# Hyena norm ahead of the output projection, output tiles added from PSUM, output weights' low parts by DMA, query statistic by column sums

## The chip, the cores and the metric

The kernel runs on one core of a Trainium2 chip. A core has five engines that work through their own instruction queues: TensorE (PE in the profile, its weight loads PEld), VectorE (DVE), ScalarE (ACT), GpSimd (POOL) and SyncE (SP), which here only issues transfers. PE writes its results to PSUM, a memory of eight banks of 128 x 512 floats; everything else lies in SBUF. The metric is device time in microseconds (us) of one execution, as the median of several.

## The reference

One layer of an encoder on 512 tokens of width 1024, in float32. What matters here:

```
h = RMSNorm(x);  proj = h @ w_in      -> q-latent (768), kv-latent (256), shared rope key (32), Hyena x0, x1, v (3 x 512)
q = RMSNorm(c_q) @ w_uq;  k, v = RMSNorm(c_kv) @ w_ukv;  per-head RMSNorm of q and k, rope, softmax attention (8 heads)
y_hyena = x0 * long_conv(x1 * v)
y_mix = concat(RMSNorm(y_attn) * g_a, RMSNorm(y_hyena) * g_h)
x = x + y_mix @ w_out
x = x + (silu(g) * u) @ w_down        (gated MLP with a width-3 convolution)
x = x + sigmoid(x @ w_ple_gate) * RMSNorm(p @ w_ple)
```

RMSNorm divides by sqrt(mean(x^2) + 1e-6). Its scale is one number per token.

## The kernel before, in words

All matrices are kept transposed: 128 features on the partitions, 512 tokens along the row. A product of float32 values is made of three matmuls: each operand is split into a rounded high part `h` and the rest, the low part `l`, and h*h, h*l and l*h are summed (`prod3`). `split` (129) does this with one ACT copy and one DVE instruction.

Weights come as a stream of tiles of 128 x 1024 (`stream`, 149 to 157), always three tiles ahead of use. `wload` (137) takes one tile: SP fetches it raw (`wr`, 2 buffers), ACT rounds it into `wh` (3 buffers), and the low part `wl` (3 buffers) is made in one of two ways. Columns below `cut` are made by DVE as raw minus high (143). For columns above `cut`, ACT writes the negative rounded weights (145), and a transfer issued by POOL (146) fetches the same weights from DRAM once more and adds them on top. For the output weights `w_out` the cut is 512 of 1024.

PE's order is the order of the program, mixed by hand: `advance` and `spawn` put small tasks between the large products when a counted time is reached. The order on the other engines is made by a planner that takes what is ready by priority; `tc.high_priority` with the numbers of `PRI` shifts instructions ahead (positive) or back (negative). Tiles of PSUM come from two pools of four banks each, `mm_ps` and `ax_ps`; a tile waits until the one that had its bank is done with.

Around the change, in order of time:

- The first products: two kv-latent tiles (482) and the rope key by `in_gemm(2)` (495), all in `mm_ps`. Their evacuation (509, 511) waits for R1, the 1/rms of x. Then come twelve Hyena tiles (619) and six q-latent tiles (639), whose squares are added up in `accx`.
- `query_scale` (672): a matmul with ones adds `accx` over the partitions, eight equal rows of 512; `rows` copies eight rows to SBUF (667, ACT, priority 500); `turn_rows` (228) transposes them on PE into 32 columns, four token blocks of eight heads; `rms_cols` makes the statistic from them. `key_task` (686) does the same for the key's squares: sums by 688 and 690, a copy by 667, transposes. Both tasks run between the steps of the query projection (763).
- `gate` (827): for each of four tiles PE transposes the long convolution's result, DVE multiplies it into `x0`, ACT squares, POOL adds the squares in `acch`, and `x0` is split with the gain g_h (845, priority -300).
- The attention loop (981) with steps n = 0 to 36: scores of step n, transposes of the probabilities of step n-3 (`turn`), product with v (`weigh`), head output (`finish`). Gates stand at n = 4, 6, 7 and 9. At n = 10 `rms_bcast` (998) makes Rh, the 1/rms of the Hyena output, with a ones matmul (220) and `rsqrt` (203). At n = 16, 24 and 32 `hyena_out` (923) makes an output tile of the Hyena half; five more follow the loop. Since Rh is one number per token, it is applied after the projection: DVE multiplies the result by Rh (928) and adds x (929).
- Four output tiles before the end, Ra is made for the attention half in the same way (1005); its tiles are normed before the projection (1008), and 1016 adds the products of the attention half to the residual.

Of the kernel before, what the change touches and what calls it, by code (L numbers as in the profile page):

```python
# [14 lines left out]
AF = mybir.ActivationFunctionType  # L15
ALU = mybir.AluOpType
# [3 lines left out]
P = 128  # L20
# [19 lines left out]
D_RC = 1.5  # L40
# [7 lines left out]
TAIL = 'E0 P E1 R O S0 S1 V0 V1 S2 S3 V2 G0 V3'  # L48
ENG = {'pr0': 'G', 'a53': 'V', 'a64': 'V', 'sp3': 'V', 'pr2': 'G', 'sp7': 'G', 'qa2': 'V', 'm5': 'V', 'a51': 'G', 'ah1': 'G', 'hl0': 'V', 'fwo': 'G', 'ah3': 'G', 'qa5': 'V', 'hl2': 'G', 'qa3': 'V', 'm6': 'V', 'm7': 'G', 'm2': 'V', 'qa1': 'V', 'sp5': 'G', 'xt': 'V', 'Uc': 'G', 'sp4': 'G', 'w01': 'V', 'w11': 'V', 'a61': 'G', 'pr3': 'G', 'a67': 'G', 'a63': 'V', 'u4': 'G', 'a65': 'G', 'w10': 'G', 'u3': 'G', 'sp0': 'G', 'eos': 'V', 'vx': 'A', 'vl': 'V', 'vh': 'V', 'va': 'V', 'vf': 'V', 've': 'V', 'vc': 'A', 'sx': 'A', 'sl': 'V', 'sh': 'V', 'sa': 'V', 'sf': 'V', 'se': 'V', 'sc': 'V', 'qa4': 'G', 'sp6': 'V', 'm4': 'V', 'rot2': 'G', 'cv5': 'V', 'm1': 'G', 'a62': 'V', 'rot1': 'G'}
ATT = {'pr', 'a', 'ah', 'hl', 'xt'}  # L50
PRI = {'rows': 500, 'val': 20, 'kt': 60, 'rms': -120, 'cols': 400, 'H': 0, 'gate': 150, 'uT': -120, 'io': -20, 'sq': 20, 'turn': 0, 'so': -300, 'fold': -120, 't8': 0, 'gsq': -50, 'ie': 400}
QACT = 1
UQ = (2, 0, 4, 3, 5, 1)
D_KS = 5.0
# [3 lines left out]
RPRI = 0  # L58
LAG = 3
NPR = 4  # L60
FILLS = (16, 24, 32)
GN = (4, 6, 7, 9)
CPRI = 50
EPS = 1e-6
# [22 lines left out]
def tile_encoder_block(  # L87
# [9 lines left out]
    def e(key, default):  # L97
        if key.rstrip("0123456789") in ATT:
            return {"V": V, "G": G}[ENG.get(key, default)]
        return V  # L100

    def pri(key):
        return tc.high_priority(offset=PRI[key]) if PRI.get(key) else nullcontext()

# [9 lines left out]
    def mm_ps():  # L114
        return psm.tile([P, T], F32, tag="mm", name="mm")

    def ax_ps():
        return psx.tile([P, T], F32, tag="ax", name="ax")

    def atile(dt=F32R):  # L120
        return apool.tile([P, T], dt, tag="a", name="a")
# [4 lines left out]
    def f32(ap):  # L126
        return ap.bitcast(F32)

    def split(hi, lo, src, g=None):
        if g is None:  # L130
            S.activation(hi, src, AF.Copy)
            V.tensor_tensor(lo, src, f32(hi), op=ALU.subtract)
        else:
            S.activation(hi, src, AF.Copy, scale=g)
            V.scalar_tensor_tensor(lo, src, g, f32(hi), op0=ALU.mult, op1=ALU.subtract)

    def wload(src, n, cut):
        raw = wpool.tile([P, 1024], F32, tag="wr", name="wr", bufs=2)
        SP.dma_start(raw[:, :n], src)
        hi = wpool.tile([P, 1024], F32R, tag="wh", name="wh", bufs=3)  # L140
        lo = wpool.tile([P, 1024], F32R, tag="wl", name="wl", bufs=3)
        S.activation(hi[:, :n], raw[:, :n], AF.Copy)  # L142
        V.tensor_tensor(lo[:, :cut], raw[:, :cut], f32(hi[:, :cut]), op=ALU.subtract)  # L143
        if cut < n:
            S.activation(lo[:, cut:n], raw[:, cut:n], AF.Copy, scale=-1.0)
            G.dma_start(lo[:, cut:n], src[:, cut:n], accum_op=ALU.add)  # L146
        return hi, lo

    stream = [(w_in[m], 1024, 1024 if m < 5 else 512) for m in range(21)]
    stream += [(w_ukn, 1024, 512)] + [(w_uq[m], 768, 384) for m in UQ] + [(w_ukv, 1024, 512)]  # L150
    stream += [(w_out[g, m], 1024, 512) for g in (1, 0) for m in range(4)]
    stream += [(w_up[m], 1024, 1024) for m in range(2 * NFF)]
    for m in range(8):
        stream += [(w_down[m][:, o * P : (o + nk) * P], nk * P, nk * P) for o, nk in ((0, 8), (8, 8), (16, 6))]
# [37 lines left out]
    def pcol(name, i=0, p0=0, p1=P):  # L192
        return par[p0:p1, POFF[name] + i : POFF[name] + i + 1]

    ident = const.tile([P, P], F32, tag="ident", name="ident")
    ones = const.tile([P, P], F32, tag="ones", name="ones")
# [6 lines left out]
    def rsqrt(out, v, w, src, n, key):  # L203
        if ENG.get("v" + key, "A") == "A":
            S.activation(out, src, AF.Ln, scale=1.0 / n, bias=eps)
            S.activation(v, src, AF.Identity, scale=1.0 / n, bias=eps)
        else:
            V.tensor_scalar(v, src, 1.0 / n, EPS, op0=ALU.mult, op1=ALU.add)
            S.activation(out, v, AF.Ln)
        S.activation(out, out, AF.Exp, scale=-0.5)  # L210
        if ENG.get("s" + key, "A") == "A":
            S.activation(w, out, AF.Square)
        else:
            V.tensor_tensor(w, out, out, op=ALU.mult)
        V.scalar_tensor_tensor(w, v, -0.5, w, op0=ALU.mult, op1=ALU.mult)
        V.scalar_tensor_tensor(out, w, 1.5, out, op0=ALU.add, op1=ALU.mult)

    def rms_bcast(out, ssq, n, tmp, key):
        ps = ax_ps()
        PE.matmul(ps, ones, ssq, start=True, stop=True)  # L220
        with pri("rms"):
            rsqrt(out, tmp(), tmp(), ps, n, key)


    def col(name="col"):
        return const.tile([P, 32], F32, tag=name, name=name, bufs=6 if name == "col" else 1)

    def turn_rows(rows):
        ps = ax_ps()
        for t in range(4):  # L230
            PE.transpose(ps[:, t * 8 : (t + 1) * 8], rows[:, t * P : (t + 1) * P], ident[0:8, 0:8])
        return ps[:, 0:32]

    def rms_cols(out, ps, n, more=None):
        v, w = col(), col()
        with pri("cols"):
            if more is not None:
                V.tensor_tensor(w, more, more, op=ALU.mult)
                V.tensor_tensor(w, ps, w, op=ALU.mult)
                ps = w  # L240
            rsqrt(out, v, col(), ps, n, "c")
# [13 lines left out]
    def tmp(dt=F32):  # L255
        return ft.tile([P, T], dt, tag="t", name="t", bufs=NTMP)
# [55 lines left out]

    def in_gemm(m):
        w = wtiles(next_w(), 8)
        ps = mm_ps()
        for k in range(0, 8, 2):
            mms(ps, prod3(w[k : k + 2], xs[k : k + 2]), start=k == 0, stop=k == 6)
            advance(T_IN / 4)
        return ps
# [60 lines left out]
    H = {}  # L380
# [283 lines left out]
    def rows(ps):  # L664
        r = tmp()[0:8, :]
        with pri("rows"):
            S.activation(r, ps[0:8, :], AF.Copy)
        return r

    qs = col("qs")  # L670

    def query_scale():
        ps = ax_ps()
        PE.matmul(ps[0:8, :], ones[:, 0:8], accx, start=True, stop=True)
        q, r1 = rows(ps), col("r1")
        yield D_RC
        V.tensor_copy(r1, turn_rows(R1[0:8, :]))
        rms_cols(qs, turn_rows(q), 768, r1)
        V.tensor_tensor(qs, qs, r1, op=ALU.mult)


    wk = next_w()
# [135 lines left out]
        rms_cols(v, turn_rows(ssq_rows[0]), 96, qs)  # L818
        V.scalar_tensor_tensor(v, v, 96.0 ** -0.5, qs, op0=ALU.mult, op1=ALU.mult)

    yh = []
    acch = xpool.tile([P, T], F32, tag="x", name="x")

    spare = [tmp]
# [2 lines left out]
    def gate(c):  # L827
        ps = mm_ps()
        for b in range(4):
            PE.transpose(ps[:, b * P : (b + 1) * P], yt[b][:, c * P : (c + 1) * P], ident)  # L830
        pb = ps.rearrange("p (a b) -> p a b", a=4)
        with pri("gate"):
            V.tensor_tensor(even_blocks(x0[c]), even_blocks(x0[c]), pb[:, 0:2, :], op=ALU.mult)
            V.tensor_tensor(odd_up(x0[c]), odd_up(x0[c]), pb[:, 2, :], op=ALU.mult)
            V.tensor_tensor(odd_down(x0[c]), odd_down(x0[c]), pb[:, 3, :], op=ALU.mult)
        with pri("gsq"):
            if c == 0:
                S.activation(acch, x0[c], AF.Square)
            else:
                sq = spare[0]()  # L840
                S.activation(sq, x0[c], AF.Square)
                e("ah%d" % c, "G").tensor_tensor(acch, acch, sq, op=ALU.add)
        with pri("so"):
            h, l = atile(), atile()
            split(h, l, x0[c], pcol("g_oh", c))
            yh.append((h, l))

    pend = []

# [49 lines left out]
    def tmp1():  # L899
        return at.tile([P, T], F32, tag="t", name="t", bufs=3)  # L900
# [22 lines left out]
    def hyena_out(m):  # L923
        ps = out_mm(m, 1, yh)
        xt = xpool.tile([P, T], F32, tag="x", name="x")
        SP.dma_start(xt, xT[m // 2][:, (m % 2) * T : (m % 2 + 1) * T])
        t = tmp1()
        V.tensor_tensor(t, ps, Rh, op=ALU.mult)
        e("xt", "G").tensor_tensor(xt, xt, t, op=ALU.add)
        xm.append(xt)  # L930

    def turn(n):
# [48 lines left out]
    for n in range(NU + LAG + 2):  # L981
        if n < NU:
            if n % 4 == 0 and 1 < n // 4 + 1 < NH:
                prep(n // 4 + 1, ap_ if n // 4 % 2 == 0 else hp)
            if n >= 4:
                scores(n)
        d = n - LAG
        if 0 <= d < NU:
            turn(d)
        d -= 1  # L990
        if 0 <= d < NU and d % 2 == 1:
            weigh(d // 4, (d % 4) // 2)
            if d % 4 == 3:
                finish(d // 4)
        if n in GN and len(yh) < 4:
            gate(len(yh))
        if n == NRH:
            rms_bcast(Rh, acch, 512, tmp1, "h")
        if n in FILLS and fill < 8:
            hyena_out(fill)  # L1000
            fill += 1
    while fill < 8:
        if fill == 8 - RFILL:
            with tc.high_priority(offset=RPRI):
                rms_bcast(Ra, acc5, 512, tmp1, "a")
                for j in range(4):
                    a, b = atile(), atile()
                    V.tensor_tensor(ys[j], ys[j], Ra, op=ALU.mult)
                    split(a, b, ys[j], pcol("g_oa", j))
                    ya.append((a, b))  # L1010
        hyena_out(fill)
        fill += 1
# [286 lines left out]
```

## Time and profile before

| | us |
|---|---|
| median of 3 runs | 758.63 (757.56 to 759.36) |
| the profiled execution | 757.62 |
| its span | 755.8 |
| PE busy | 723.0 (96%) |
| DVE busy | 504.8 (67%) |
| ACT busy | 373.1 (49%) |
| POOL busy | 151.7 (20%) |

A row of a timeline names the start and the length in us, the engine, the line, the operation and what it writes and reads; in brackets stands how long the engine was idle before it, and what released it. A row of a table of stretches gives, for each engine, busy us and the number of instructions, then the TensorE clock that was granted (1.00 is full speed), the share of the DMA engines that was in use, and GB/s. A row of groups gives busy us and the mean length in ns.

### The profile page before, as it was taken

The page shows a single profiled execution, that of the slowest core. Times are in us where ns is not written, and L with a number is a line of the kernel's source. Part 1 is how long each engine was busy: PE and PEld are TensorE (multiplying, and loading weights), DVE is VectorE, ACT ScalarE, POOL GpSimd, SP SyncE. Part 2 cuts the span into 40 slices and gives each one's busy share as a digit, 9 for nine tenths or more (in the row PEclk, how much of TensorE's full clock was granted, in tenths as well). Part 3 has the DMA queues.
Part 4 walks back from the last instruction along what each step waited for, and adds up shares of the span by engine and source line. Part 5 has one row for each costly group of instructions (what it writes and reads, how often), then busy time and mean ns, then how long its engine had stood idle before and what let it go on. Part 6 is the DMA issues. An engine that isn't in the chain of part 4 may idle for free.

```text
span 755.8 us, 9037 instructions
## 1 busy us (share of the span) xinstructions
PE 723.0 (96%) x3254; PEld 582.7 (77%) x3254; DVE 504.8 (67%) x780; ACT 373.1 (49%) x575; POOL 151.7 (20%) x150
## 2 busy tenths in 40 slices
PE   6999999996997899999999999999999999999997
PEld 4767888874665777788888888888888888888886
DVE  6499988888779987885766566666665332233482
ACT  7465545467668896564534444444353222126340
POOL 2111101110126662130422222222122000005000
PEclk9999999997999999999999999999999999999999
DMA  8765744443636210533232323232323233323331
GB/s 279 239 153 128 191 128 91 106 94 77 147 91 170 71 25 19 126 103 106 83 113 84 112 84 112 83 104 92 106 89 92 82 109 101 98 90 127 111 112 56
DMA packets 30110, 82.83 MB, mean 110 GB/s; under 512 B 3913, under 2 KB 5257, under 8 KB 30066
## 3 DMA queue, kind: packets, MB, share of 16 engines
q1 hardware_dynamic: 24418, 71.62, 31.2%
q0 software_dynamic: 5392, 10.25, 7.2%
q10 hardware_dynamic: 256, 0.39, 0.2%
q8 instruction: 25, 0.41, 0.2%
q14 instruction: 19, 0.16, 0.1%
HBM read 77.00 MB, written 2.10 MB: 105 GB/s over the span
## 4 chain that ended last, share of the span: by engine, by line
PE 54%; DVE 0%; ACT 0%; DVEq 0%; issue 0%
PE mm L176 37%; PE ax L176 17%; PE ax L220 0%; DVE t L1127 0%; ACT t L1126 0%; DVEq L1294 0%; DVE t L1128 0%
## 5 line engine op out<-in xcount | busy, mean ns | idle before, releaser
L176 PE MATMUL mm<-a,wh 128*128 128x512 f32 (+1 forms) x928 | 288.8, 392 | 9.2 <-ACT wh L273 6.4
L176 PEld LDWEIGHTS mm<-a,wh 128*128 128x128 f32 x928 | 174.3, 190 | 51.2 <-issue 6.5
L143 DVE TENSOR_TENSOR wl<-wr,wh 128x1024 fp32r<-128x1024 f32 (+3 forms) x113 | 124.3, 1101 | 113.8 <-ACT wh L142 111.8
L142 ACT ACTIVATE wh<-wr 128x1024 fp32r<-128x1024 f32 (+1 forms) x113 | 116.5, 1031 | 158.0 <-PE mm L176 121.6
L176 PE MATMUL mm<-a,wl 128*128 128x512 f32 (+1 forms) x464 | 180.7, 389 | 0.0
L176 PE MATMUL ax<-a,wh 128*128 128x512 f32 x384 | 118.3, 389 | 0.0
L176 PEld LDWEIGHTS mm<-a,wl 128*128 128x128 f32 x464 | 88.1, 190 | 17.8 <-DVE wl L274 0.2
L176 PEld LDWEIGHTS ax<-a,wh 128*128 128x128 f32 x384 | 72.1, 188 | 14.9
L176 PE MATMUL mm<-g,wh 128*128 128x512 f32 x232 | 73.8, 400 | 1.7 <-ACT t L647 1.7
L176 PE MATMUL ax<-a,wl 128*128 128x512 f32 x192 | 74.7, 389 | 0.0
L1063 POOL TENSOR_TENSOR f<-f 128x512 f32<-128x512 f32 x22 | 28.7, 1303 | 169.2 <-DVE f L543 149.5
L176 PE MATMUL mm<-h,wh 128*128 128x512 f32 x192 | 59.0, 389 | 0.0
L176 PEld LDWEIGHTS mm<-g,wh 128*128 128x128 f32 x232 | 44.2, 192 | 13.7 <-ACT t L647 2.1
L176 PE MATMUL mm<-g,wl 128*128 128x512 f32 x116 | 46.1, 397 | 0.0
L176 PEld LDWEIGHTS ax<-a,wl 128*128 128x128 f32 x192 | 36.0, 188 | 7.6
L176 PEld LDWEIGHTS mm<-h,wh 128*128 128x128 f32 x192 | 36.0, 188 | 7.5
L1059 DVE TENSOR_TENSOR f<-mm,R 128x512 f32<-128x512 f32 x22 | 15.2, 691 | 33.7 <-PE mm L176 33.7
L176 PE MATMUL mm<-h,wl 128*128 128x512 f32 x96 | 37.3, 389 | 0.0
L1062 ACT ACTIVATE f<-f 128x512 f32<-128x512 f32 x22 | 13.9, 631 | 44.8 <-DVE f L543 44.8
L536 ACT ACTIVATE f<-f,par 128x512 f32<-128x512 f32 x44 | 35.5, 808 | 1.0 <-DVE f L1059 1.0
L543 DVE SCALAR_TENSOR_TENSOR f<-f,par 128x511 f32<-128x511 f32 x44 | 33.9, 771 | 1.4
L146 POOL DMA_DIRECT2D wl<-in_w_in_dram x16 | 13.9, 868 | 103.8 <-DVE wl L143 53.5
(312 smaller groups left out, 1015.1 us busy)
## 6 DMA issues: line engine op xcount, KB each, us to landing
wr<-in_w_up_dram SPq DMA_DIRECT2D x44, 512.0 KB, 3.5
wr<-in_w_in_dram SPq DMA_DIRECT2D x19, 512.0 KB, 3.9
wr<-in_w_down_dram SPq DMA_DIRECT2D x16, 512.0 KB, 3.5
x<-in_xT_dram SPq DMA_DIRECT2D x16, 256.0 KB, 4.2
wl<-in_w_in_dram POOLq DMA_DIRECT2D x16, 256.0 KB, 5.3
wr<-in_w_out_dram SPq DMA_DIRECT2D x8, 512.0 KB, 4.4
wr<-in_w_gate_dram SPq DMA_DIRECT2D x8, 512.0 KB, 3.6
wr<-in_w_down_dram SPq DMA_DIRECT2D x8, 384.0 KB, 3.1
```

The source lines that it names most:

```text
L142: S.activation(hi[:, :n], raw[:, :n], AF.Copy)
L143: V.tensor_tensor(lo[:, :cut], raw[:, :cut], f32(hi[:, :cut]), op=ALU.subtract)
L146: G.dma_start(lo[:, cut:n], src[:, cut:n], accum_op=ALU.add)
L176: last = PE.matmul(out, l, r, start=start and i == 0, stop=stop and i == n - 1)
L536: S.activation(c, z, AF.Identity, scale=pcol(w, 3 * m + 1), bias=pcol(b, m))
L543: V.scalar_tensor_tensor(c[:, 0 : T - 1], z[:, 1:T], pcol(w, 3 * m + 2), c[:, 0 : T - 1], op0=ALU.mult, op1=ALU.add)
L1059: V.tensor_tensor(z, ps_up.pop(m), R2, op=ALU.mult)
L1062: S.activation(cc[0], cc[0], AF.Silu)
L1063: G.tensor_tensor(cc[1], cc[0], cc[1], op=ALU.mult)
```

## The change

- `hyena_norm` is new and takes the place of the statistic at n = 10. It makes 1/rms in a PSUM tile (`rms_psum`, with the square on ACT and the last steps of DVE in PSUM), multiplies each gated tile by it into another PSUM tile, and splits that one. `gate` no longer splits.
- `hyena_out` adds its product from PSUM to the residual directly; the multiplication with Rh is gone. The splits' priority goes from -300 to -20, and the three output tiles in the loop move from steps 16, 24, 32 to 18, 25, 31.
- Ra is made by `rms_psum` as well.
- The cut of `w_out` goes from 512 to 0: the whole low part of these eight tiles comes by DMA.
- `query_scale` takes `accx` block by block as the weights of a matmul with eight columns of ones, which gives the 32 columns directly; the copy, the wait of 1.5 in the counted time and the second set of transposes go.
- The rope key's product (`in_gemm(2)`) takes its tile from `ax_ps`.

```diff
-PRI = {..., 'so': -300, ...}
+PRI = {..., 'so': -20, ...}
-FILLS = (16, 24, 32)
+FILLS = (18, 25, 31)
...
-        V.tensor_tensor(lo[:, :cut], raw[:, :cut], f32(hi[:, :cut]), op=ALU.subtract)
+        if cut:
+            V.tensor_tensor(lo[:, :cut], raw[:, :cut], f32(hi[:, :cut]), op=ALU.subtract)
...
-    stream += [(w_out[g, m], 1024, 512) for g in (1, 0) for m in range(4)]
+    stream += [(w_out[g, m], 1024, 0) for g in (1, 0) for m in range(4)]
...
+    def rms_psum(out, ssq, n, tmp, ps, last=None):
+        PE.matmul(ps, ones, ssq, start=True, stop=True)
+        v = tmp()
+        with pri("rms"):
+            V.tensor_scalar(v, ps, 1.0 / n, EPS, op0=ALU.mult, op1=ALU.add)
+            S.activation(out, v, AF.Ln)
+            S.activation(out, out, AF.Exp, scale=-0.5)
+            S.activation(ps, out, AF.Square)
+            V.scalar_tensor_tensor(ps, v, -0.5, ps, op0=ALU.mult, op1=ALU.mult)
+            V.scalar_tensor_tensor(out if last is None else last, ps, 1.5, out, op0=ALU.add, op1=ALU.mult)
...
     def in_gemm(m):
-        ps = mm_ps()
+        ps = ax_ps() if m == 2 else mm_ps()
...
     def query_scale():
+        r1 = col("r1")
+        V.tensor_copy(r1, turn_rows(R1[0:8, :]))
         ps = ax_ps()
-        PE.matmul(ps[0:8, :], ones[:, 0:8], accx, start=True, stop=True)
-        q, r1 = rows(ps), col("r1")
-        yield D_RC
-        V.tensor_copy(r1, turn_rows(R1[0:8, :]))
-        rms_cols(qs, turn_rows(q), 768, r1)
+        for t in range(4):
+            PE.matmul(ps[:, t * 8 : (t + 1) * 8], accx[:, t * P : (t + 1) * P], ones[:, 0:8], start=True, stop=True)
+        rms_cols(qs, ps[:, 0:32], 768, r1)
         V.tensor_tensor(qs, qs, r1, op=ALU.mult)
+        yield None
...
     def gate(c):
-        with pri("so"):
-            h, l = atile(), atile()
-            split(h, l, x0[c], pcol("g_oh", c))
-            yh.append((h, l))
+        gated.append(c)
+
+    def hyena_norm():
+        rps = mm_ps()
+        rms_psum(Rh, acch, 512, tmp1, rps, rps)
+        for c in range(4):
+            with pri("so"):
+                ps = mm_ps()
+                V.tensor_tensor(ps, x0[c], rps, op=ALU.mult)
+                h, l = atile(), atile()
+                split(h, l, ps, pcol("g_oh", c))
+                yh.append((h, l))
...
     def hyena_out(m):
-        t = tmp1()
-        V.tensor_tensor(t, ps, Rh, op=ALU.mult)
-        e("xt", "G").tensor_tensor(xt, xt, t, op=ALU.add)
+        V.tensor_tensor(xt, xt, ps, op=ALU.add)
...
         if n == NRH:
-            rms_bcast(Rh, acch, 512, tmp1, "h")
+            hyena_norm()
...
-                rms_bcast(Ra, acc5, 512, tmp1, "a")
+                rms_psum(Ra, acc5, 512, tmp1, ax_ps())
```

More of the change, by code (lines that the diff above doesn't have):

```diff
@@ L50 @@
 ATT = {'pr', 'a', 'ah', 'hl', 'xt'}
-PRI = {'rows': 500, 'val': 20, 'kt': 60, 'rms': -120, 'cols': 400, 'H': 0, 'gate': 150, 'uT': -120, 'io': -20, 'sq': 20, 'turn': 0, 'so': -300, 'fold': -120, 't8': 0, 'gsq': -50, 'ie': 400}
+PRI = {'rows': 500, 'val': 20, 'kt': 60, 'rms': -120, 'cols': 400, 'H': 0, 'gate': 150, 'uT': -120, 'io': -20, 'sq': 20, 'turn': 0, 'so': -20, 'fold': -120, 't8': 0, 'gsq': -50, 'ie': 400}
 QACT = 1
@@ L819, in softmax_scale @@
         V.scalar_tensor_tensor(v, v, 96.0 ** -0.5, qs, op0=ALU.mult, op1=ALU.mult)
-    yh = []
+    yh, gated = [], []
     acch = xpool.tile([P, T], F32, tag="x", name="x")
@@ L994, in tile_encoder_block @@
                 finish(d // 4)
-        if n in GN and len(yh) < 4:
-            gate(len(yh))
+        if n in GN and len(gated) < 4:
+            gate(len(gated))
         if n == NRH:
-            rms_bcast(Rh, acch, 512, tmp1, "h")
+            hyena_norm()
         if n in FILLS and fill < 8:
```

## The prediction

> **What bounds the kernel now.** I first read the chain that ended last, then a table of stretches, then the idle places of TensorE (PE) in the timeline.
>
> ```profile
> by line: PE mm L176 36.9%; PE ax L176 17.3%; PE ax L220 0.2%; DVE t L1127 0.1%; ACT t L1126 0.1%; DVE t L1128 0.0%; DVEq L1294 0.0%; issue 0.0%
> ```
>
> The chain is nothing but matmuls, and its first piece starts at 340 us. Behind that point lie the feed-forward part and the gate, which the change does not touch.
>
> ```profile
> core 0: us, PE busy (x) PEld busy (x) DVE busy (x) ACT busy (x) POOL busy (x), PEclk, DMA share, GB/s
> 180.00:190.00 10.00, 7.99 (x22) 4.69 (x22) 6.84 (x17) 7.10 (x15) 0.86 (x1) 0.52 0.11 23
> ...
> 220.00:290.00 70.00, 61.33 (x369) 49.83 (x368) 65.14 (x154) 59.81 (x128) 44.47 (x49) 1.00 0.32 81
> 300.00:340.00 40.00, 39.59 (x170) 31.30 (x168) 34.85 (x49) 22.82 (x33) 9.30 (x8) 1.00 0.45 107
> 340.00:751.00 411.00, 410.83 (x1831) 340.29 (x1830) 219.88 (x255) 159.54 (x202) 67.81 (x51) 1.00 0.31 98
> ```
>
> From 340 us PE idles 0.2 us in 411, so whatever happens earlier moves the end by as much. From 300 to 340 it idles 0.4 us. What can be won lies in two places: around 180 us, where PE waits and then runs at a granted clock of 0.52, and in the attention loop (220 to 290), where VectorE (DVE) is busy 93% of the time and PE idles 8.7 us. The change also touches one place near 35 us.
>
> **Query statistic.** Engines work through their queues in order; PE's order is that of the program.
>
> ```profile
> 171.08 1.02 PE L674 MATMUL ax<-accx,ones 128*8 128x512 f32 x2
> ...
> 172.51 0.62 PE L176 MATMUL mm<-g,wh 128*128 128x512 f32 x2
> ...
> 173.87 0.63 PE L176 MATMUL ax<-t,sel 128*8 128x512 f32 x2
> ...
> 175.82 0.41 PE L231 MATMUL ax<-ident,R 8*128 8x8 f32 x4
> 182.01 0.59 PE L231 MATMUL ax<-ident,t 8*128 8x8 f32 x4 [5.79 <-ACT t L667]
> 182.53 1.87 PE L690 MATMUL ax<-qr,ones 32*8 32x512 f32 x2
> ...
> 190.04 0.73 PE L176 MATMUL mm<-g,wh 128*128 128x512 f32 x2
> ```
>
> ```profile
> 181.39 0.57 ACT L667 ACTIVATE t<-ax 8x512 f32<-8x512 f32 x1
> 182.06 0.63 ACT L131 ACTIVATE a<-t 128x512 fp32r<-128x512 f32 x1
> ...
> 185.19 0.57 ACT L667 ACTIVATE t<-ax 8x512 f32<-8x512 f32 x1
> ```
>
> The sums of L674 were there at 172.1, but ScalarE (ACT) copied them only at 181.4, behind the splits of the spectrum tiles. PE stood 5.79 us and then ran at half clock until about 189.6. The change drops this copy and the transposes behind it: four pairs of column sums write the statistic where the transposes put it.
>
> ```profile
> L220 PEld LDWEIGHTS ax<-accx,ones x2: 187/190/193, 26.4 to 26.6; 128*128 128x128 f32 x2
> ```
>
> Each now loads a 128x128 block as weights: 8 loads of 0.19 are 1.5 us, with 8 columns to stream behind each, in place of 1.02 and 0.59 us: even. Then PE goes on to L690 and two steps of the query projection (1.36 us each, 172.51 to 173.87), and meets the next thing of the same kind: the transposes of the key rows, behind the second copy (185.19 in the old order). PE gets there near 180.2 (0.8 us later than the old order up to 175.82, plus 1.0 for L690 at full clock and 2.7 for two steps). The copy is ready to go from 177.5 on, but ACT's queue decides: at best it takes the old place of the first copy and ends at 182.0, at worst it stays where it was and ends at 185.8. With the transposes (0.35) PE resumes at 182.3 to 186.1, where it resumed at 190.04: 7.7 to 3.9 us earlier. From that goes what the clock then costs: one slow window of 3.4 us costs 1.7 us (the row is in the next part), two cost 3.4. So the bounds are 0.5 and 7.7; I take the middle place (184.25, 5.8 earlier) with one slow window: **-4.1 us**. DVE's part of the chain behind (sums, key scale) is paced by PE, so this is carried on to the loop.
>
> **The shared key in the other PSUM pool (line 495).**
>
> ```profile
> 32.71 0.39 PE L176 MATMUL mm<-a,wl 128*128 128x512 f32 x1
> 34.96 0.70 PE L176 MATMUL mm<-a,wh 128*128 128x512 f32 x2 [1.86 <-DVE x L509]
> ...
> 40.81 1.12 PE L220 MATMUL ax<-accy,ones 128*128 128x512 f32 x2
> ```
>
> ```profile
> 40.08 0.68 DVE L523 TENSOR_TENSOR accy<-accy,t 128x512 f32<-128x512 f32 x1
> ```
>
> ```profile
> 35.99:39.40 3.41, 3.41 (x10) 2.64 (x9) 1.84 (x5) 2.72 (x5) 0.88 (x1) 0.50 0.39 91
> ```
>
> With a fifth tile elsewhere, the projection at 34.96 no longer waits for L509 and its 18 matmuls end near 37.0. But the next matmul, L220, needs L523, which ends at 40.8 by DVE and ACT alone. So 1.86 us of idle become 3.7 a little later, and the slow window moves behind it: of the window from 39.4 to 42.8, the 2.0 us after 40.8 run at half clock and lose 1.0. Before, the slow window fell where PE would have waited anyway.
>
> ```profile
> 50.05 1.06 ACT L142 ACTIVATE wh<-wr 128x1024 fp32r<-128x1024 f32 x1 [2.60 <-PE mm L176]
> ```
>
> The next wait (0.9 us near 53.6, for the filter's sine) hides nothing of it, since ACT's queue ahead of that sine waits for PE here. I take **+1.0 us**; bounds +1.7 (a whole slow window) and -1.9 (if the planner also moves L523 forward).
>
> The Trainium skill, "TensorE: Matmul & The Clock Gate" (Part 1), has the clock halved after one idle window of about 3.4 us that runs freely. The trace differs: half clock at 35.99 after only 1.86 us of idle. By the rule as it stands this term would be 0, and the sum below -6.3 instead of -5.3.
>
> **The attention loop.** Of the stretch from 215 to 297, grouped by line and form:
>
> ```profile
> L135 DVE SCALAR_TENSOR_TENSOR a<-x,par,a 128x512 fp32r<-128x512 f32 x4 | 5.5, 1368 | 0.0
> ...
> L134 ACT ACTIVATE a<-x,par 128x512 fp32r<-128x512 f32 x4 | 2.9, 715 | 0.0
> ...
> L928 DVE TENSOR_TENSOR t<-mm,Rh 128x512 f32<-128x512 f32 x3 | 2.1, 685 | 1.0 <-PE mm L176 1.0
> ...
> L215 DVE SCALAR_TENSOR_TENSOR t<-t 128x512 f32<-128x512 f32 x1 | 1.8, 1756 | 0.0
> L143 DVE TENSOR_TENSOR wl<-wr,wh 128x512 fp32r<-128x512 f32 x2 | 1.7, 866 | 0.0
> ```
>
> ```profile
> L135 DVE SCALAR_TENSOR_TENSOR g<-mm,par,g x6: 741/744/751, 125.9 to 160.0; 128x512 fp32r<-128x512 f32 x6
> ```
>
> DVE, piece by piece. The four Hyena low parts read PSUM now: 5.5 us become 4 x 0.744 = 3.0 (-2.5). New are four products x0 times 1/rms into PSUM; no row writes PSUM from DVE, so I take L928's 0.685 (+2.7; 1.4 if it went twice as fast, 5.5 at half the speed). Three output tiles lose their product (-2.1), two weight tiles lose L143 (-1.7). The Hyena statistic runs as three DVE steps through PSUM instead of four: L215 at 1.76 becomes 0.69 and one of 0.69 goes to ACT (-1.7). Together -5.3 us of 65. ACT gains two half-width copies and a square, about 1.5 us, in a queue that is 85% full. The slow ones among the removed are worth most:
>
> ```profile
> 238.84 0.93 PE L176 MATMUL ax<-ks,qs 96*128 96x512 f32 x3 [2.93 <-DVE ptl L132]
> ```
>
> This wait follows the one L135 that took 2.94 us (median 0.77) while POOL worked on SBUF. The Trainium skill, "SBUF — State Buffer" (Who interferes with whom), says that a DVE instruction with two SBUF inputs contends with a GpSimd instruction that reads SBUF, one with a single such input does not; 2.94 against 0.744 agrees.
>
> Half of -5.3 should show, as DVE, ACT and PE are all over 85% busy: -2.6. Against it stands a new order: the output tile at the loop's 18th step (was 16th) now needs the normed tiles, and so the statistic, which only its evacuation needed before.
>
> ```profile
> 242.52 1.02 PE L220 MATMUL ax<-x,ones 128*128 128x512 f32 x2
> ...
> 261.03 0.60 PE L941 MATMUL ax<-ident,pr 128*128 128x128 f32 x4
> ```
>
> ```profile
> 259.69 0.67 DVE L216 SCALAR_TENSOR_TENSOR Rh<-t,Rh 128x512 f32<-128x512 f32 x1
> ```
>
> The old statistic took from 242.5 to 260.4, and PE is at its 18th step at 261. Behind it now come product, ACT half and DVE half (0.69 + 0.72 + 0.74) for the first tile and 1.43 of DVE for each further one: PE may wait up to 3.3 us at the output tile. Behind it in PE's queue stand the scores and transposes of the next steps, and softmax waits for those; but three steps of softmax are in hand, and DVE does needed work meanwhile. I charge one refill, 0.7. **Sum -1.9 us**, bounds -5.3 and +3.
>
> **Behind the loop.** Five output products and four halves of L143 leave DVE, but PE is full there; it idles 0.4 us, on DVE. **-0.3 us.** The low parts are now whole 512 KB transfers on POOL's queue.
>
> ```profile
> 320.47 0.86 POOL L146 DMA_DIRECT2D wl<-in_w_out_dram x1 [4.80 <-ACT wl L145]
> ```
>
> ```profile
> 329.27 0.39 PE L176 MATMUL ax<-a,wl 128*128 128x512 f32 x1
> ```
>
> ```profile
> DMA to landing us min/median/max: 3.7/5.2/8.8
> ```
>
> The last one is issued at 320.5 and used at 329.5. It comes 0.4 later (ACT's copy is twice as wide) and takes longer by its second half: as queue 0 moves 10.25 MB in 7.2% of the span, 256 KB more is 1.4 us. 320.5 + 0.4 + 5.2 + 1.4 = 327.5: on time, cover 2.0 us. At the longest landing it would be 1.6 late, for one tile.
>
> **Sum:** -4.1 + 1.0 - 1.9 - 0.3 = -5.3 on the profiled execution's own 757.62, so 752.3. The median of the runs shown is 1.0 above that execution: **753.3 us**.
>
> **Rivals.**
> - *The wait only moves* (the change doesn't do what it says). The key rows' copy stays at 185.2 with two slow windows behind it: -0.5 instead of -4.1, other terms as above: -1.7, 756.9 us. For it: ACT's queue is full of splits until 182.7. Against it: the copy has a high priority and its input is there 7 us earlier.
> - *All of it arrives.* The copy comes early (-7.7, less one slow window, -6.0), the loop gains DVE's whole 5.3, and the early term is 0: -11.6, 747.0 us. For it: the 2.93 us wait goes as a whole. Against it: PE has only 8.7 us of idle there, and ACT gets more work.
> - *Slower: PE stands at the first output tile.* If each step of the new chain waits in its queue as the old ones did (six steps in 17.9 us, 3.0 each), nine steps end at 269.5 and the other three tiles 4.3 later; with 0.7 for the last matmuls that is 274.5, where the tile would have ended near 264.2 unhindered: 10.3 us of standing and a slow window (1.7), against 5.3 of DVE work saved. Then -4.1 + 1.0 - 0.3 + 6.7 = +3.3, 761.9 us. It decides from about 7 us of standing. Against it: the new products and splits stand close behind the statistic in priority (20 instead of 300 later).
>
> **How the numbers follow.** My forecast has 0.60, with its own range 749.5 to 756.5; the moved wait 0.17, all of it 0.14, slower 0.09. The range reaches from 747.5 to 758.5: the low end leaves half of the second rival out, the high end is the first with the early term's +1.7 and a small stall, and leaves the third out. A change within 0.2% (1.5 us: 757.1 to 760.1) can't be told from none. Faster: the forecast, the second rival and half of the first, 0.83; same: the other half, 0.09; slower 0.08.
>
> **What would show it.** Right: no wait of PE on L667's successor longer than 5 us near 180, PE at the key transposes by 186; the low parts of the Hyena tiles near 0.74 us each; a short PE wait at the first output tile; a PE idle of 3 to 4 us near 37 with a slow window behind. Wrong: PE standing over 7 us in the loop near 260, DVE writing PSUM at over 1 us, or a wait for a low part by DMA behind 310.

## The result, and the profile after

The changed kernel takes 769.56 us (median of four executions, 768.57 to 771.94), the kernel before 758.33 (of four, 757.56 to 759.36): the ratio is 1.0157, with a 95% interval of 1.0145 to 1.017. It is slower by 11 us; forecast was 753.3, with a range of 747.5 to 758.5. The profiled execution took 768.57 us, its span is 766.8.

From the page of the changed kernel, the busy times (share of the span, instructions) and the chain that ended last:

```profile
PE 725.1 (95%) x3256; PEld 584.7 (76%) x3256; DVE 495.1 (65%) x766; ACT 377.1 (49%) x576; POOL 150.9 (20%) x150
...
PE mm L177 36%; PE ax L177 17%; PE ax L221 0%; DVE t L1148 0%; ACT t L1147 0%; DVEq L1315 0%; DVE t L1149 0%
```

PE still sets the end, and DVE did lose its work: 495.1 us busy where it had 504.8. The time went where PE stands or runs at a lower clock. The table of stretches of the changed kernel (columns as before: us, then busy us and number of instructions of PE, PEld, DVE, ACT and POOL, granted clock, DMA share, GB/s):

```profile
39.50:50.50 11.00, 9.78 (x18) 5.58 (x19) 7.82 (x13) 4.80 (x7) 0.86 (x1) 0.53 0.22 47
186.00:194.00 8.00, 3.77 (x12) 3.11 (x13) 7.12 (x22) 6.27 (x16) 0.00 (x0) 0.57 0.47 110
251.00:262.00 11.00, 4.19 (x16) 3.79 (x17) 8.15 (x13) 4.60 (x9) 1.39 (x2) 0.53 0.06 13
```

```profile
220.00:300.00 80.00, 65.79 (x379) 53.36 (x378) 65.83 (x160) 63.02 (x133) 43.36 (x48) 0.94 0.32 79
...
350.00:762.00 412.00, 411.83 (x1835) 340.84 (x1833) 220.79 (x255) 159.56 (x202) 68.43 (x52) 1.00 0.31 98
```

and the attention loop in the kernel before:

```profile
220.00:300.00 80.00, 70.65 (x423) 57.67 (x421) 71.31 (x166) 64.53 (x136) 45.87 (x51) 1.00 0.28 72
```

In 80 us of the loop all three engines did less than before, PE 379 instructions for 423: an engine that became full would show the opposite. PE's timeline shows the waits (in brackets the idle time and what ended it):

```profile
40.72 2.08 PE L221 MATMUL ax<-accy,ones 128*128 128x512 f32 x2 [3.32 <-DVE accy L536]
...
165.85 0.73 PE L177 MATMUL mm<-g,wh 128*128 128x512 f32 x2 [1.65 <-ACT t L660]
...
175.57 1.06 PE L690 MATMUL ax<-ones,accx 128*128 128x8 f32 x8
...
180.27 1.02 PE L704 MATMUL ax<-qr,ones 32*8 32x512 f32 x2
...
190.23 0.59 PE L244 MATMUL ax<-ident,t 8*128 8x8 f32 x4 [5.99 <-ACT t L680]
...
213.17 0.41 PE L244 MATMUL ax<-ident,t 8*128 8x8 f32 x4 [0.68 <-ACT t L680]
217.77 0.49 PE L177 MATMUL ax<-ks,qs 96*128 96x512 f32 x1 [1.25 <-ACT ks L761]
231.39 0.63 PE L962 MATMUL ax<-ident,a 128*128 128x128 f32 x4 [1.43 <-DVE st L888]
...
257.81 1.22 PE L177 MATMUL mm<-pth,g 128*128 128x256 f32 x4 [8.14 <-DVE a L135]
...
269.54 0.70 PE L177 MATMUL mm<-a,wh 128*128 128x512 f32 x2
...
307.95 0.74 PE L177 MATMUL mm<-pth,g 128*128 128x256 f32 x4 [0.69 <-ACT pth L131]
```

Four of these rows have a counterpart in every kernel here, and cut a span into five stages: the first query projection (165.85), the last set of 8x8 transposes (213.17), the third transposes of probabilities, the first that wait for DVE (231.39), and the last product with v (307.95). In the table, "start" runs up to the first of them, "query" to the second, "heads" to the third, "loop" to the fourth, "rest" to the end (profiled executions, us).

| kernel | start | query | heads | loop | rest | span |
|---|---|---|---|---|---|---|
| before | 161.7 | 49.4 | 17.2 | 67.8 | 459.7 | 755.8 |
| after | 165.8 | 47.3 | 18.2 | 76.6 | 458.8 | 766.8 |
| difference | +4.1 | -2.1 | +1.0 | +8.7 | -0.9 | +11.0 |
| forecast | +1.0 | -4.1 | 0 | -1.9 | -0.3 | -5.3 |

**The loop** holds most of it. PE stood 8.14 us, not at the output tile (269.54: no wait) but before, at a product with v whose operands were ready. It waited for DVE's split (L135), that is, for a tile of the `mm` pool to be given back. DVE's and ACT's timelines at this place:

```profile
253.09 0.69 DVE L234 SCALAR_TENSOR_TENSOR mm<-t,mm 128x512 f32<-128x512 f32 x1 [0.46 <-ACT mm L233]
253.82 0.70 DVE L235 SCALAR_TENSOR_TENSOR mm<-mm,Rh 128x512 f32<-128x512 f32 x1
254.56 1.89 DVE L866 TENSOR_TENSOR mm<-x,mm 128x512 f32<-128x512 f32 x3
256.36 1.40 DVE L135 SCALAR_TENSOR_TENSOR a<-mm,par,a 128x512 fp32r<-128x512 f32 x2
257.68 0.68 DVE L866 TENSOR_TENSOR mm<-x,mm 128x512 f32<-128x512 f32 x1
```

```profile
247.39 0.62 ACT L231 ACTIVATE Rh<-t 128x512 f32<-128x512 f32 x1
...
251.79 0.64 ACT L232 ACTIVATE Rh<-Rh 128x512 f32<-128x512 f32 x1
252.46 0.60 ACT L233 ACTIVATE mm<-Rh 128x512 f32<-128x512 f32 x1
255.29 1.88 ACT L134 ACTIVATE a<-mm,par 128x512 fp32r<-128x512 f32 x3 [2.22 <-DVE mm L866]
```

The statistic's tile and three products hold all four banks. By the code the fourth product (257.68) then takes the bank that the first split gives back, and PE's next one the second: PE starts 0.05 us after the end of DVE's second split (257.76). From PE's stop at 249.67 the row of single steps goes on without it: exponential and square on ACT, two steps and three products on DVE, two splits on both. From 252.6 on softmax, which should have filled DVE and ACT meanwhile, was waiting for PE. Then the clock was low until 261.9. The statistic itself came late: its logarithm (L231) was done at 248.0, its exponential (L232) started at 251.79, with softmax and copies ahead of it in ACT's queue. No run here changes its priority (`rms`, -120), so what an earlier statistic would save is not shown.

### The profile page after: what moved, and what is told of

Read it like the earlier page. It is cut to its first block, busy times and chain, and to the rows that moved or that the text cites. A ratio compares the mean times of both kernels' runs of the same rounds, so it can differ in the third digit from the quotient of the medians.

```text
span 766.8 us, 9015 instructions
## 1 busy us (share of the span) xinstructions
PE 725.1 (95%) x3256; PEld 584.7 (76%) x3256; DVE 495.1 (65%) x766; ACT 377.1 (49%) x576; POOL 150.9 (20%) x150
## 4 chain that ended last, share of the span: by engine, by line
PE 54%; DVE 0%; ACT 0%; DVEq 0%; issue 0%
PE mm L177 36%; PE ax L177 17%; PE ax L221 0%; DVE t L1148 0%; ACT t L1147 0%; DVEq L1315 0%; DVE t L1149 0%
## 5 line engine op out<-in xcount | busy, mean ns | idle before, releaser
L177 PE MATMUL mm<-a,wh 128*128 128x512 f32 (+1 forms) x912 | 283.7, 393 | 7.5 <-ACT wh L286 5.6
L177 PEld LDWEIGHTS mm<-a,wh 128*128 128x128 f32 x912 | 171.6, 190 | 49.3 <-ACT wh L286 5.6
L144 DVE TENSOR_TENSOR wl<-wr,wh 128x1024 fp32r<-128x1024 f32 (+3 forms) x105 | 118.4, 1129 | 114.5 <-ACT wh L142 112.5
L177 PE MATMUL mm<-a,wl 128*128 128x512 f32 (+1 forms) x456 | 177.3, 389 | 0.0
L177 PE MATMUL ax<-a,wh 128*128 128x512 f32 x400 | 123.1, 389 | 0.0
L177 PEld LDWEIGHTS ax<-a,wh 128*128 128x128 f32 x400 | 75.0, 188 | 15.5
L177 PE MATMUL ax<-a,wl 128*128 128x512 f32 x200 | 77.8, 389 | 0.0
L177 PE MATMUL mm<-g,wh 128*128 128x512 f32 x232 | 73.2, 397 | 1.7 <-ACT t L660 1.7
L177 PEld LDWEIGHTS mm<-g,wh 128*128 128x128 f32 x232 | 43.9, 191 | 12.8 <-ACT t L660 2.1
L177 PEld LDWEIGHTS ax<-a,wl 128*128 128x128 f32 x200 | 37.6, 188 | 7.9
```

Of the source, the lines that this page charges most:

```text
L177: last = PE.matmul(out, l, r, start=start and i == 0, stop=stop and i == n - 1)
```

## The experiments

A ratio stands against the kernel before, timed together with the run, with its 95% interval. Times of different runs are compared by their ratios.

### The parts alone

The query part alone:

```diff
 before +  query_scale(): column sums of accx, no copy, no D_RC, no second transposes
```

> The kernel before with the new query statistic alone. Theory: the standing near 176 to 182 moves to the key rows' copy, which keeps its place in ScalarE's queue; TensorE resumes 3.6 us earlier, loses 1.6 to a slow window and gives some back at the next copy: 755.5 to 757.5. Rival, the gain is given back in full before the attention loop: 758 to 759.

Measured: 758.61 us, ratio 0.9987 (0.9974 to 1.0). PE's timeline:

```profile
189.23 0.59 PE L231 MATMUL ax<-ident,t 8*128 8x8 f32 x4 [6.00 <-ACT t L667]
```

The wait of 5.79 us ahead of the query's transposes is gone, and one of 6.00 stands ahead of the key's. The query stage took 48.9 us for 49.4 before (in the longest of ten executions, 760.30): the wait moved, as the prediction's first rival had it, and the time is in the range of this run's rival.

The low parts alone:

```diff
-    stream += [(w_out[g, m], 1024, 512) for g in (1, 0) for m in range(4)]
+    stream += [(w_out[g, m], 1024, 0) for g in (1, 0) for m in range(4)]
```

> The kernel before with the output weights' low parts by DMA alone. Theory: hidden; two weight tiles leave VectorE in the attention loop, worth at most 1 us: 757.3 to 758.5. Rival, the doubled transfers come late behind 310: over 759.5, with TensorE waiting on a DMA.

Measured: 759.04 us, ratio 1.0007 (0.9988 to 1.0026): no difference, between the two expectations. The profiled execution was the longest of ten (764.64), so its stages are not compared. No wait of PE in it ends on a transfer of a low part.

The rope key's tile alone:

```diff
-        ps = mm_ps()
+        ps = ax_ps() if m == 2 else mm_ps()
```

> The kernel before with the rope key's tile in the second PSUM pool alone. Theory: the wait moves from 33 to 37 and grows to 3.3 us, and three slow windows follow it in nearly every run: the query projection starts 3 to 4 us later, 760.5 to 762.5. Rival, chance: as often as in the kernel before, 758 to 760.

Measured: 762.90 us (760.48 to 763.88), ratio 1.0048 (1.0031 to 1.0064). PE's timeline of this kernel:

```profile
42.65 2.08 PE L220 MATMUL ax<-accy,ones 128*128 128x512 f32 x2 [4.54 <-DVE accy L523]
```

The wait at 35 us is gone, one of 4.54 stands ahead of L220, and the clock is low from 41 to 51. The time is just above the range of the theory.

The Hyena part alone (statistic, products, splits and their priority, output tiles; Ra is made as in the kernel before):

```diff
 before +  rms_psum, hyena_norm, gated; 'so': -20; FILLS = (18, 25, 31); hyena_out adds from PSUM
```

> The kernel before with the Hyena part alone (norm ahead of the projection through PSUM, output tiles added from PSUM, steps 18, 25 and 31, priority -20). Theory: the 8.1 us of standing in the loop and the slow window behind it are this part's own; the stretch from the first attention wait to the end of the loop takes 76 us where it took 67.8: 766 to 768. Rival, it needs the other parts: under 763.

Measured: 766.08 us, ratio 1.0101 (1.0083 to 1.012). PE's timeline:

```profile
253.37 1.22 PE L176 MATMUL mm<-pth,g 128*128 128x256 f32 x4 [8.69 <-DVE a L135]
```

The same stand, in a loop of 75.9 us (67.8 before), as the theory had it. By ratio the four parts alone are -1.0, +0.5, +3.6 and +7.7 us: +10.8, with about 2.6 us of uncertainty between them, where the whole gave +11.9. Ra by `rms_psum` is in the whole but in none of the four; no run shows it alone.

### Parts taken back out of the changed kernel

```diff
 after, but in_gemm(2) in mm_ps() again
```

> The changed kernel, with the rope key's product back in the first PSUM pool. Theory: the wait of 1.9 us near 33 comes back, the 3.3 us near 37 and three slow windows behind it go, and the first matmul of the query projection starts 4.1 us earlier: 765 to 766. Rival, the slow windows fall by chance: they stay, and the time is within 1.5 us of 769.6.

```diff
 after, but rms_bcast for Rh, splits inside gate at -300, FILLS = (16, 24, 32), hyena_out multiplies by Rh
```

> The changed kernel without its Hyena part (splits in the gates at -300, the statistic applied after the projection, output tiles at steps 16, 24, 32), with the query sums, the low parts by DMA, the rope key's tile and the attention statistic through PSUM kept. Theory: the Hyena part costs 8 to 10 us and the rest of the change about 0 to 2 more than the kernel before: 759 to 761.5. Rival, the cost is spread over the parts: 763 or more.

Measured: 767.82 us without the key tile (ratio 1.011, 1.0089 to 1.0131), 766.88 without the Hyena part (1.0096, 1.0069 to 1.0124). The first time lies between its two expectations, the second is in the rival's range. By ratio the first is 3.6 us less than the changed kernel, what the key tile costs alone; the second is 4.6 less, where the Hyena part costs 7.7 alone, a difference of 3.1 with an uncertainty of 2.7. In the first the start fell to 162.5 us, but the 8.14 us at the loop stayed. In the second the 8.14 were gone and the loop fell to 70.9 us, but PE waited at the first output tile for a split that came late:

```profile
263.51 0.51 PE L177 MATMUL mm<-a,wh 128*128 128x512 f32 x1 [1.99 <-ACT a L134]
265.94 0.79 PE L177 MATMUL mm<-a,wh 128*128 128x512 f32 x1 [1.92 <-DVE a L135]
```

and four stretches at a low clock cost more than in the changed kernel (summed over half-microsecond stretches, PE's busy time times what the clock lacked: 12.8 us against 8.6). So what the Hyena part costs alone is not what its removal returns: another wait and the slow stretches behind it take some of the room. Why the planner put this split late is not shown.

### What the stand in the loop is

One tile of PSUM for all four products, so that banks are free:

```diff
+        ps = mm_ps()
         for c in range(4):
             with pri("so"):
-                ps = mm_ps()
                 V.tensor_tensor(ps, x0[c], rps, op=ALU.mult)
```

> The changed kernel, with one PSUM tile for the four normed products in turn in place of four tiles. Theory of the banks: the 8.1 us for which TensorE stands near 250 is a wait for a PSUM bank, since the statistic and three products hold all four banks of their pool; with two held, TensorE goes on at 249 and the standing is under 2 us there. The four products now run one after another, so a wait of up to 3 us may appear at the first output tile. Time 761 to 765 (5 to 9 us below the 769.6 of the changed kernel). Rival, the late chain: the statistic comes too late whatever the banks; then TensorE stands over 5 us at the first output tile and the time is above 767.

Measured: 767.56 us, ratio 1.0108 (1.0087 to 1.0128). PE's and ACT's timelines:

```profile
258.36 1.22 PE L177 MATMUL mm<-pth,g 128*128 128x256 f32 x4 [5.34 <-ACT pth L131]
```

```profile
254.90 0.69 ACT L134 ACTIVATE a<-mm,par 128x512 fp32r<-128x512 f32 x1 [2.23 <-DVE mm L866]
257.14 0.69 ACT L134 ACTIVATE a<-mm,par 128x512 fp32r<-128x512 f32 x1 [1.55 <-DVE mm L866]
257.72 0.59 ACT L131 ACTIVATE pth<-ax 128x512 fp32r<-128x512 f32 x1
```

The wait at the product of step 13 is gone, as the theory of the banks had it. But PE goes two steps further and waits 5.34 us at the product of step 15, now for ACT's copy of its own transposes: in ACT's queue two splits stand ahead of it that wait for the products. The same chain blocks, through a queue in place of a bank. The time is in the rival's range, but PE does not wait at the first output tile, where the rival had it.

The splits' priority back at -300, with the four tiles and with the one:

```diff
-'so': -20,
+'so': -300,
```

> The changed kernel with the priority of the Hyena products and splits at -300, as in the kernel before, all else as changed. Theory of the queue order: what stops TensorE near 250 is that ScalarE and VectorE hold the steps of the Hyena norm, each of which waits for the other engine, ahead of the softmax of the next steps; pushed back, they fall between softmax work, the 8.1 us go, and TensorE waits at the first output tile instead, for 1 to 4 us: 762 to 765. Rival, the banks alone: the four tiles hold their banks as long or longer, the wait near 250 stays over 6 us: 768 to 771.

> The changed kernel with one PSUM tile for the four normed products in turn and the priority of these products and splits at -300. Each of the two alone left a standing of 5.3 and 8.1 us near 250. Theory that both causes act, banks first and then queue order: with banks free the low priority can take effect, the standing near 250 falls under 2 us, and TensorE waits 1 to 5 us at the first output tile: 762 to 766. Rival, the serial chain has to be paid wherever it stands: the sum of the waits between 245 and 275 stays over 6 us, 766 to 769.

Measured: 768.61 us (ratio 1.0127, 1.0095 to 1.0159), with 8.14 us at the same place; and 770.54 (1.0154, 1.0139 to 1.0169), with 5.35. Both theories fell. The first is in its rival's range: with four tiles the lower priority leaves the order as it was. With one tile it leaves the first two splits ahead of the softmax copy at 259.18 and puts the third one behind later copies, 3.7 us later than it was with one tile alone (259.59, in a timeline that was 1.5 us ahead):

```profile
264.73 0.68 ACT L134 ACTIVATE a<-mm,par 128x512 fp32r<-128x512 f32 x1
```

The stand stays, and PE waits another 1.02 and 0.28 us at the first output tile for the fourth split. The sum of the waits is over 6 us, as the rival said; the time is above its range too.

The same work further on in the order, in two places:

```diff
         if n == NRH:
             hyena_norm()                  # the statistic alone, left in SBUF
+        if 14 <= n < 18:                  # second place: steps 18 to 21
+            hyena_tile(n - 14)            # one product and its split
-FILLS = (18, 25, 31)
+FILLS = (20, 25, 31)                      # second place: (23, 27, 31)
```

> The changed kernel, but the statistic alone stands at step 10 (it is left in SBUF, so its PSUM tile is given back), the four products and splits follow one per step at steps 14 to 17, and the first output tile in the loop stands at step 20 (was 18). Theory (the place of issue, not the work, makes TensorE stand): no wait of TensorE over 3 us between 235 and 275 us, the stretch from the first to the last of the compared waits in the loop falls from 76.6 to 71 us or less, and the median lies between 762 and 766 us, against 769.6 for the changed kernel. Rival (the serial chain has to be paid wherever it stands): TensorE waits 5 us or more at a product with v of steps 14 to 19 or at the output tile of step 20, and the median lies between 767.5 and 771.

> The changed kernel with the statistic alone at step 10, the products and splits one per step at steps 18 to 21, and the three output tiles at steps 23, 27 and 31. The statistic ended at 262.4 us with TensorE at step 16 in the run with steps 14 to 17, so at step 18 the products find their factor ready. Theory (place): no wait of TensorE over 2 us between 235 and 290 us, last compared wait in the loop 68 to 70 us behind the first (72.4 with steps 14 to 17, 67.8 in the kernel before), median 761 to 763.5. Rival (added work on ACT and DVE): the stretch stays at 71.5 us or more and the median at 764 to 766.

Measured: 765.04 us (ratio 1.0087, 1.0072 to 1.0102) and 765.51 (1.0088, 1.0061 to 1.0115). PE's timeline, first place and second place:

```profile
262.59 0.86 PE L177 MATMUL mm<-pth,g 128*128 128x256 f32 x4 [3.67 <-DVE Rh L235]
```

```profile
273.67 0.74 PE L177 MATMUL mm<-pth,g 128*128 128x256 f32 x4 [1.78 <-ACT pth L131]
275.41 0.80 PE L177 MATMUL mm<-ptl,g 128*128 128x256 f32 x4 [1.00 <-DVE ptl L132]
```

The loop took 72.4 and 73.3 us for 76.6. So about half of its 8.7 us (4.2 in the first place, 3.3 in the second) came from issuing everything at once at step 10: the first run's median is in the range that this gave, its wait and its loop a little above. The rest stayed in both places; the second run came out as its rival said, and the idea that all of it is a matter of place fell. In the second place the stand is broken into smaller waits, with splits that wait for products again ahead of the copies in ACT's queue:

```profile
269.67 0.69 ACT L134 ACTIVATE a<-mm,par 128x512 fp32r<-128x512 f32 x1 [0.93 <-DVE mm L866]
...
271.78 1.35 ACT L134 ACTIVATE a<-mm,par 128x512 fp32r<-128x512 f32 x2 [0.67 <-DVE mm L866]
273.03 0.59 ACT L131 ACTIVATE pth<-ax 128x512 fp32r<-128x512 f32 x1
```

That these handovers make up the whole remainder, rather than the added work on ACT, isn't settled.

### What the key tile and the key rows' copy cost, and what they could bring

The key tile alone, with the kv-latent's statistic 4 us later in the counted time of PE's order:

```diff
 e11, and
-D_LR = 7.0
+D_LR = 11.0
```

> The kernel before with the rope key's product in the second PSUM pool and the kv-latent sum moved 4 us of matmuls back in TensorE's order. Theory: the wait near 33 goes and none takes its place, as the sum now stands where its input is there; no slow window near 36 to 48: the query projection starts 2 to 4 us earlier, 755 to 757.5. Rival, another input (the weights of the next product, or the filter's sine) is late instead and takes the gain: 758 to 760.

Measured: 763.24 us (759.62 to 765.25), ratio 1.0049 (1.0029 to 1.0068), no less than the key tile alone. That is above both expectations. Its profile (of the shortest of ten executions, 759.62) has no wait ahead of L220 and no low clock between 30 and 62 us, but a new wait behind:

```profile
75.75 1.65 PE L176 MATMUL ax<-g 128*128 128x512 f32 x6 [3.63 <-DVE g L414]
```

L414 makes a low part of what the filter's last sine layer gives. So another input is late there, as the rival had it, and the start takes 162.4 us, no less than the 161.7 before. What made most executions longer than this one, no profile shows.

The query part alone, with the key's transposes 4 and 6.5 us later in the counted time of PE's order:

```diff
 e3, and
-D_RC = 1.5
+D_RC = 5.5        # second kernel: 8.0
```

> The kernel before with the new query statistic and the key rows' transposes 4 us of matmuls later in TensorE's order. Theory: TensorE works on the query projection while ScalarE comes to the copy, the standing falls from 6.0 to under 2 us and no slow window follows; the key's chain then starts at the same time as with the query statistic alone, so the gain arrives at the attention loop only where TensorE is not waiting for that chain: 753 to 757. Rival, the chain of the key decides when the scores start: 757.5 to 759.5.

> The kernel before with the new query statistic and the key rows' transposes two further steps later (8.0 in the counted time, where 5.5 left 3.9 us of standing). Theory: the standing falls under 1.5 us, no slow window follows, 752 to 754.5. Rival, the key's chain now reaches the scores later: TensorE waits there, 754.5 to 757.

Measured: 754.71 us (752.09 to 757.95), ratio 0.9944 (0.992 to 0.9969), and 754.49 (750.40 to 756.39), ratio 0.9958 (0.9941 to 0.9974). Both beat the kernel before; the second step later brought nothing that the intervals show. PE's timelines:

```profile
187.87 0.59 PE L231 MATMUL ax<-ident,t 8*128 8x8 f32 x4 [3.89 <-ACT t L667]
```

```profile
187.31 0.41 PE L231 MATMUL ax<-ident,t 8*128 8x8 f32 x4 [1.18 <-ACT t L667]
```

The first wait is longer than the 2 us that was expected, the second is as expected. The copy comes no earlier; PE does steps of the projection meanwhile. The query stage falls to 45.1 and 44.0 us, from 49.4, in the shortest execution of each.

The rest of the change on top of that, without the key tile, with the products in the first and in the second of the later places:

```diff
 e13 (e15), with in_gemm(2) in mm_ps() and D_RC = 5.5
```

> As the run before, with the rope key's tile back in the first pool and the transposes of the key rows 4 us later in TensorE's order. Theory (place of issue; the key tile costs 4 us; the later key turn brings 4 us): 753 to 758 us, below the kernel before or even with it. Rival (chain has to be paid): 759 to 764 us.

> As the run before, with the rope key's tile back in the first pool and the key transposes 4 us later. Theory (place): 753.5 to 756.5 us. Rival (added work): 757.5 to 760.

Measured: 758.63 us (ratio 1.0002, 0.9993 to 1.0012) and 760.45 (1.0025, 1.0014 to 1.0036). The first lies between its two expectations, the second above both. Neither reaches the 754.7 of the query part with a later key turn: the Hyena part with the low parts and Ra still costs about 4 us in the better place, and going later doesn't return it. The loop took 72.3 and 73.2 us, as with the other parts around it.

## Why the prediction was wrong

**The loop's term failed, by 10.6 us of the 16.3 that are missing** (the sum was 752.3 on the profiled execution's own time, and it took 768.57). Its prices were right:

```profile
L135 DVE SCALAR_TENSOR_TENSOR a<-mm,par,a 128x512 fp32r<-128x512 f32 x4 | 2.9, 744 | 0.1
L866 DVE TENSOR_TENSOR mm<-x,mm 128x512 f32<-128x512 f32 x4 | 2.6, 690 | 0.0
```

The splits from PSUM took 744 ns as taken over, the products into PSUM 690 ns where 685 was assumed. The step that failed is "PE may wait up to 3.3 us at the output tile ... I charge one refill, 0.7". It priced the chain by when its last result reaches the output tile. But the new instructions stand in order with others: they take PSUM tiles at step 10 and so hold up the product with v of step 13, long before the tile that needs them. PE stood 8.14 us there, and the loop took 8.7 us longer where 1.9 less were said; with the tiles later in the order (steps 14 to 17) 4.2 of these went. How much of DVE's relief, -2.6 in the sum, arrived can't be told apart from the standing. Neither the forecast nor the slower rival asked who else takes tiles from that pool. That rival was near in size (10.3 us of standing and a slow stretch; 8.14 and a slow stretch came) but had the wrong place: it named the first output tile, which never waited in the changed kernel. The sign that the prediction set for itself, PE standing over 7 us in the loop, came.

**The query's term was the rival's.** The prediction counted PE's way to the key's transposes well: 18.5 us behind the first query projection, and PE stopped 18.4 behind it (190.23 less 5.99 less 165.85). What failed is "I take the middle place" for the copy. ACT's timeline:

```profile
188.88 0.63 ACT L131 ACTIVATE t<-accy 128x512 fp32r<-128x512 f32 x1
189.59 0.59 ACT L680 ACTIVATE t<-ax 8x512 f32<-8x512 f32 x1
```

The copy started 23.7 us behind the first query projection, 23.5 in the kernel before. Its sums were there at 181.3; a priority of 500 did not bring it past the splits. That is the worse of the prediction's two bounds, worth 0.5 us by it; alone the part brought 1.0 (0 to 2.0), and the query stage of the changed kernel is 2.1 shorter.

**The key tile's term had the right mechanism and the wrong size:** +1.0 was said, +3.6 (2.4 to 4.9) came, beyond the bound of 1.7. "Idle of 3 to 4 us near 37" is there, 3.32. The clock is what was mis-sized: one window of 3.4 us was counted, of which 2.0 after the start of the matmul that waits (L220 before, L221 after), and in the changed kernel it was low from 40.05 to 50.3, three windows, with PE busy from 40.72 on. The Trainium skill, "TensorE: Matmul & The Clock Gate" (Part 1), has the clock back at full after one busy window of about 3.4 us. The trace does not agree here: PE was busy all through the second window (43.5 to 46.9), and the third was still at half clock. By that rule this term would have been below what was said, so it would have misled further.

**Heads:** +1.0 was not in the sum. The first scores waited 1.25 us for the split of a key piece (217.77), 0.20 in the kernel before. That split waited for a transfer. ACT's timeline, before and after:

```profile
213.97 0.63 ACT L747 ACTIVATE ks<-kr 96x512 fp32r<-96x512 f32 x1 [1.55 <-DMA kr<-x]
```

```profile
217.09 0.63 ACT L761 ACTIVATE ks<-kr 96x512 fp32r<-96x512 f32 x1 [2.59 <-DMA kr<-x]
```

From the list of transfers of the changed kernel (KB each, us to landing):

```profile
wl<-in_w_in_dram POOLq DMA_DIRECT2D x16, 256.0 KB, 5.3
...
wl<-in_w_out_dram POOLq DMA_DIRECT2D x8, 512.0 KB, 7.3
...
kr<-x ACTq DMA_DIRECT2D x1, 128.0 KB, 7.1
...
kr<-x ACTq DMA_DIRECT2D x1, 64.0 KB, 6.3
```

The larger low parts were used in time, as said (6.6 us was the estimate of their landing), and no wait of PE ends on them. But the two transfers of the key piece (`kr`) landed after 7.1 and 6.3 us, where they took 6.1 and 5.3 before; a low part was issued at 207.5, 2.1 us ahead of the first. In the nine kernels with the larger low parts and the key's transposes at their old place the first took 6.9 to 7.4 us and the scores waited 1.19 to 1.50; in the five without them 6.1 to 6.5 and 0.20 to 0.66. So the larger transfers make the key piece late. In the time of the kernel with the low parts alone no cost shows.

**Behind the loop** -0.3 was said, -0.9 came.

The chances put 0.83 on faster because the early term, the query and the loop were each given a value between bounds, and each time the outcome lay at the bad end or beyond it.

## What to carry to other kernels

When work is put ahead of a product, ask which pool its tiles come from and whose tiles are queued behind them: a serial chain holds up the next user of its banks and of its engines' queues, not only its own consumer. A wait for something that another queue orders was won here by giving the waiting engine other work, not by making the input ready earlier. A part that costs nothing by its instructions can cost some us by where its idle time falls, so test parts alone as well as taken out.

## What the runs showed of the hardware

- The length of a short idle time did not settle how long the clock stayed low. In the one profiled execution of each, all eight kernels with the rope key's tile in `ax_ps` and the early statistic lost 3.4 to 4.9 us of clock between 30 and 62 us (PE's busy time times what the clock lacked); of the nine others (the one with the later statistic left out, which lost none there) seven lost 0 to 1.7 and two 3.4, at about the same idle time in that stretch (2.8 to 5.0 us, against 3.7 to 5.2). In the kernels with the moved tile the first work behind the idle is L221 and a short product of the filter; that these keep the clock low was not tested by itself.
- PE's column sums, eight passes of 8 columns with a new block of weights each, took 1.06 us together (175.57), less than the 1.5 us that their weights were priced at (eight loads of 0.19).
- DVE took 0.69 to 0.70 us per 128x512 for instructions with two inputs that read PSUM and write PSUM (L234, L235, L866), about what L928 took before with its result in SBUF (0.685).
